# A decoder trunk in fp32: seven raw weight buffers instead of five, norm sums by transposing the squares, and another order of the program

## The chip, the cores and the metric

One core of one Trainium2 chip runs one program. The time is that of the device, in microseconds, from launch to the last byte of the output; 360.67 us is the median of three runs before the change (360.07 to 362.04).

## What is computed

Two layers of a decoder on 256 tokens of width 1024, all in fp32. The first mixes tokens by block attention (with 256 tokens and blocks of 256 it is plain causal attention), the second by three sparse branches: compressed keys, selected blocks, and a window (here the last two cover every earlier token). Each mixer is gated by a SiLU path, and after each layer an embedding is projected, gated by a sigmoid and added.

```python
for i in range(DEPTH):                       # DEPTH = 2
    h = rms_norm(x, norm_gain[i])
    if i % N_MIXERS == 0:
        x = x + moba_layer(h, moba_w_in[j], ..., moba_w_out[j], pos)
    else:
        x = x + nsa_layer(h, nsa_w_in[j], ..., nsa_cmp_w1[j], nsa_cmp_w2[j], nsa_w_out[j], pos)
    gate = jax.nn.sigmoid(rms_norm(x, ple_gate_gain[i]) @ ple_w_gate[i])
    x = x + gate * (p[i] @ ple_w_proj[i])
...
def rms_norm(x, gain):
    y = xf * lax.rsqrt(jnp.mean(xf * xf, axis=-1, keepdims=True) + NORM_EPS)
```

## The kernel before, in words

The residual stream lies in `xT`, eight tiles of 128 features by 256 tokens. A product in fp32 is made of three matmuls in a 32-bit format with a shorter mantissa: each operand is split into a rounded `hi` and a rest `lo`, and hi·hi + hi·lo + lo·hi is summed. For weights `split` (L490) does that: a DMA brings 512 KB (a granule, 128 x 1024) into a `raw` buffer, ScalarE writes `hi`, VectorE writes `lo = raw - hi`; there are five buffers each for raw, hi and lo (L21). A raw buffer comes free when its lo is made, a hi or lo when its matmuls are done. For activations `split_act` (L502) makes `a` from `xT`. A `Unit` (L517) is a product of 512 columns over eight such tiles, in four granules.

The sum over features of the squares, for the norm, is in class `Norm` (L592): ScalarE squares `xT`, VectorE adds the squares up in `sqacc`; `finish` (L617) then multiplies `sqacc` by a column of ones on TensorE, which sums over the 128 partitions and puts tokens on partitions, VectorE makes `ms` of it, GpSimd raises it to the power -1/2 (`rstd`), and two transposes spread that over partitions (`bc`). There are three such norms: `a` (first layer), `b` (its embedding gate), `c` (second layer).

Attention: a pair of heads has steps `A` (queries and keys transposed), `S` (scores: matmuls into two banks `s`, then on VectorE mask, scale and row extreme, which frees the bank, and the exponential on ScalarE), `T` (probabilities scaled, transposed on TensorE, copied) and `V` (times values). In the second layer the steps of group g are `gA`, `gS0` to `gS3`, `gT0` to `gT3`, `gV`; the compressed branch multiplies windows (`KC`, `KD`) by weights `in_w` in the four steps `W0` to `W3`, straight from raw buffers without a split, so that two raw buffers stay taken from the load (`w:W0`) until the step's matmuls are done.

The order. `PROGRAM` (L25) lists the steps; this is the order in which instructions are recorded and buffers of a kind are dealt out, so a load that stands early takes its buffer early. `Plan.schedule` (L264) then puts the recorded instructions into one order per engine with costs of its own (`cost`, L187; `SWITCH` for a change of TensorE's tiling, `POW` for GpSimd's power), and each engine executes its queue in that order. Nearly every instruction is emitted at L400, so the profile is read by tiles. SP issues almost all DMAs; `x0` to `x7` load the tiles of the input, `w:c0` to `w:c7` and `w:d0` to `w:d3` the first weights (eight tiles of the query's, four of the key's, 256 KB each), `consts` the constants and head gains, and `tk`, `tq` build the rotary tables from them on VectorE.

Of the kernel before, what the change touches and what calls it, by code (L numbers as in the profile page):

```python
# [7 lines left out]
F32 = mybir.dt.float32  # L8
F32R = mybir.dt.float32r
AF = mybir.ActivationFunctionType  # L10
OP = mybir.AluOpType
AX = mybir.AxisListType

P = 128
T = 256
D = 1024
KT = 8
HD = 64
EPS = 1e-6
SWITCH, POW = 150.0, 2300.0  # L20
NRAW, NHI, NLO, NPT, NA = 5, 5, 5, 9, 9  # L21
WARM = 16
MARGIN = 100.0

PROGRAM = ("w:c0 w:d0 x0 c0 x1 w:c1 w:d1 d0 c1 x2 x3 d1 w:c2 x6 w:d2 x4 x5 w:c3 w:c4 consts tk w:c5 tq w:c6 w:d3 x7 c2 a.1  "  # L25
# [21 lines left out]

WIDE = ('no',)

# [59 lines left out]
class Plan:  # L109
# [77 lines left out]
    def cost(self, op, views, first):  # L187
        n = first.elems() if isinstance(first, View) else 0
        e, m = op.engine, op.method
        if m == "dma_start":  # L190
            v = first if isinstance(first, View) else op.args[1]
            return v.elems() * 4 * v.ap.ap[0][1]
        if e == "tensor":
            k, c = op.args[1].ap.ap[0][1], op.args[1].ap.ap[1][1]
            op.mode = tuple(128 if x > 64 else 64 if x > 32 else 32 for x in (k, c))
            if m == "transpose":
                return 109.2
            if op.args[1].ap.dtype == mybir.dt.bfloat16:
                return n / 2.4
            if op.args[1].ap.dtype == F32R:  # L200
                return (n + 32) / 2.4 if n > 128 else 110

            tiles = 128 // op.mode[1] if op.mode[0] == 128 else 1
            return 2 * max(109.2 / tiles, 2 * n / 2.4 / tiles)
        if e == "gpsimd":
            if op.kwargs.get("op") == OP.pow:
                return (POW if n < 16 else 1300.0) + 130.0 * n
            return 100 + 2.3 * n
        psum = any(self.tags[v.tile.tag]["psum"] for v in views)
        rows = first.ap.ap[0][1]  # L210
        half = 110 if rows in (60, 64) and (any(v.box()[0] != first.box()[0] for v in views)
                                            or psum and first.ap.dtype == F32R and m == "activation") else 0
        if e == "scalar":
            if first.tile.tag == "early":
                return 1500.0
            c = (60 if psum else 110) + 0.833 * max(n, op.args[1].elems())
            return half + c + 93 * sum(isinstance(op.kwargs.get(k), View) for k in ("scale", "bias", "accum_out"))
        if m == "tensor_tensor_reduce":
            return 130 + 1.04 * n
        if m == "reciprocal":  # L220
            return 65 + 6.9 * n
        if m == "tensor_reduce":
            return 65 + 1.04 * op.args[1].elems()
        two = len([v for v in views if v.elems() > 2 and v is not first]) > 1
        if not psum and not two and m in ("tensor_copy", "tensor_scalar"):
            return 70 + half + 0.52 * n + 60 * any(isinstance(x, View) and x.elems() == 1 for x in op.args[2:])
        if m == "tensor_tensor" and args_step(op.args[1]) >= 16:
            return 65 + 1.75 * n
        return 65 + half + 1.055 * n + (65 if m == "scalar_tensor_tensor" and isinstance(op.args[2], View) else 0)
# [192 lines left out]
def trunk(ctx: ExitStack, tc: tile.TileContext, a, out):  # L422
# [3 lines left out]
    nc = Plan(tc.nc, {"sb": sb, "psum": psum})  # L426
# [8 lines left out]
    consts, wpool, apool, work = Pool(1), Pool(5), Pool(NA), Pool(2)  # L435
# [26 lines left out]
    ident, mask, valid, rmask = cs("ident"), cs("mask"), cs("valid"), cs("rmask")  # L462
# [7 lines left out]
    nc.vector.memset(warm, 0.0)  # L470
    neg_half = consts.tile([P, 16], F32, name="neg_half")
    nc.vector.memset(neg_half, -0.5)
    ones = consts.tile([P, 2], F32, name="ones")
    nc.vector.memset(ones, 1.0)

    def tables(name, gain, gains):
        t = work.tile([P, 2, 2, len(gains), HD], F32, tag=name[:2] + str(len(gains)), name=name, bufs=1)
# [114 lines left out]
    class Norm:  # L592
# [24 lines left out]
        def finish(self):  # L617
            ps = bank("tr", 2)
            for t in range(2):
                nc.tensor.matmul(ps[:, 2 * t:2 * t + 2], self.acc[:, 0, t * P:t * P + P], ones, start=True, stop=True)  # L620
            self.ms = work.tile([P, 2], F32, tag="ms", name="ms")
            nc.vector.tensor_scalar(self.ms, ps[:, 0:4:2], 1.0 / D, EPS, op0=OP.mult, op1=OP.add)
            self.rstd = work.tile([P, 2], F32, tag="rstd", name="rstd")
            nc.gpsimd.tensor_tensor(self.rstd, self.ms, neg_half[:, :2], op=OP.pow)
            self.e2 = work.tile([P, 2, 2], F32, tag="e2", name="e2")
            nc.vector.tensor_scalar(self.e2[:, 0], self.ms, 64 * EPS, None, op0=OP.mult)
            nc.vector.tensor_scalar(self.e2[:, 1], self.ms, EPS, None, op0=OP.mult)
            ps = bank("tr", 2)
            for t in range(2):
                nc.tensor.transpose(ps[:, t * P:t * P + P], self.rstd[:, t:t + 1].to_broadcast([P, P]), ident)  # L630
            self.bc = work.tile([P, T], F32, tag="bc", name="bc", bufs=1)
            nc.copy(self.bc, ps[:, :T])
# [230 lines left out]
    ps = bank("tr", 2)  # L863
# [4 lines left out]
    x0 = {}  # L868
# [185 lines left out]
    for k in (1, 3, 5, 6, 7):  # L1054
        todo[f"a.{k}"] = lambda k=k: nc.hold_on(lambda: n0.add(k), at["consts"])
    todo.update(a=n0.finish, consts=consts_, masks=masks_, tq=lambda: tab.update(q=tables("tq0", gmoba, [0])),
                tk=lambda: tab.update(k=tables("tk0", gmoba, [1])))
# [8 lines left out]
    x1, n2 = {}, Norm()  # L1066
# [11 lines left out]
    c2 = consts.tile([124, 2, HD], F32, name="c2")  # L1078
# [8 lines left out]
    def tabs2():  # L1087
# [4 lines left out]
                ntk=lambda: tab1.update(k=tables("tk1", gnsa, [2, 3])))  # L1092
# [304 lines left out]

    groups = [Group(g, f" {g}b" not in PROGRAM) for g in range(4)]
    for h, x in enumerate(halves1):
# [7 lines left out]
    for g in range(4):  # L1407
# [3 lines left out]
                KD0=lambda: KD(0), KD1=lambda: KD(1))  # L1411
# [6 lines left out]

    for step in PROGRAM.split():

        name, _, g = step.partition("/")
# [109 lines left out]
```

## Time and profile before

| | before |
|---|---|
| median of 3 runs | 360.67 us |
| the profiled execution | 362.55 us |
| its span | 360.7 us |
| TensorE matmuls / weight loads busy | 98% / 86% |
| VectorE, ScalarE, GpSimd busy | 89%, 75%, 7% |
| granted TensorE clock | 1.00 |
| moved by DMA | 58.95 MB, 163 GB/s |

PE and PEld are TensorE's matmuls and its weight loads, DVE is VectorE, ACT ScalarE, POOL GpSimd, SP the engine that issues DMAs. In groups and timelines a row reads: output tile <- input tiles, shape, count; behind the bar the busy time, the mean of one, and the engine's idle time ahead. `mm`, `s` and `tr` are banks of the accumulator memory. The profiled execution shows the span of the program's instructions; 1.85 us of its time lie around it.

### The profile page before, as it was taken

To read this page: it belongs to the slowest core of one execution; us is meant where nothing else is said; L and a number is where in the kernel's file an instruction comes from. 1 tells how busy PE (TensorE), PEld (TensorE's weight loads), DVE (VectorE), ACT (ScalarE), POOL (GpSimd) and SP (SyncE) were. 2 spreads that over 40 slices of the span, in tenths; PEclk is the share of its full clock that TensorE was granted. 3 is DMA by queue.
4 is the path that set the end of the run, shared out by engine and by line. 5 is a ranking of instruction groups with operands and counts; after the bars stand their busy time and mean duration, and the time that the engine had idled before them with its cause. 6 is when DMAs were issued, how large, how long until landed. Compare 5 with 4: busy or idle time off the path is not lost.

```text
span 360.7 us, 6783 instructions
## 1 busy us (share of the span) xinstructions
PE 353.6 (98%) x2397; PEld 311.2 (86%) x2397; DVE 321.7 (89%) x779; ACT 269.5 (75%) x594; POOL 25.9 (7%) x22
## 2 busy tenths in 40 slices
PE   8999999999999999999999999999999999999995
PEld 6788888989989999999889988876998888888884
DVE  4989999999999967969999989999899999878744
ACT  4867499886989966736664978987998999855731
POOL 1013300330000000000003200003000000000000
PEclk9999999999999999999999999999999999999999
DMA  7997657654533334644553664138834331136003
GB/s 226 321 367 255 196 194 271 195 177 121 171 119 116 119 118 124 224 148 149 171 164 125 231 203 150 62 109 298 300 128 160 109 125 59 60 115 224 12 6 113
DMA packets 20770, 58.95 MB, mean 163 GB/s; under 512 B 2560, under 2 KB 5632, under 8 KB 20736
## 3 DMA queue, kind: packets, MB, share of 16 engines
q1 hardware_dynamic: 20160, 58.04, 48.6%
q10 hardware_dynamic: 576, 0.48, 0.4%
q8 instruction: 19, 0.31, 0.3%
q14 instruction: 15, 0.12, 0.1%
HBM read 57.46 MB, written 1.05 MB: 162 GB/s over the span
## 4 chain that ended last, share of the span: by engine, by line
PE 72%; DVE 13%; ACT 6%; DMA 6%; issue 2%; SPq 0%; DVEq 0%; ACTq 0%
PE mm L400 55%; PE tr L400 10%; PE s L400 7%; DVE sm L400 3%; DVE lo L400 3%; DVE big L400 2%; ACT hi L400 2%; DVE hl L400 2%; DMA raw<-in_nsa_in 2%; DMA tmp<-in_moba_in 1%; DMA xT<-in_x 1%; DMA raw<-in_w 1%; DVE tmp L400 1%; ACT sm L400 1%; ACT pt L400 1%
## 5 line engine op out<-in xcount | busy, mean ns | idle before, releaser
L400 PE MATMUL mm<-hi,a 128*128 128x512 f32 (+2 forms) x448 | 128.7, 377 | 0.6 <-ACT hi L400 0.6
L400 ACT ACTIVATE hi<-raw 128x1024 fp32r<-128x1024 f32 (+2 forms) x98 | 97.5, 1007 | 37.3 <-PE mm L400 28.5
L400 DVE TENSOR_TENSOR lo<-raw,hi 128x1024 fp32r<-128x1024 f32 (+2 forms) x98 | 112.7, 1162 | 12.6 <-ACT hi L400 11.9
L400 PE MATMUL mm<-a,hi 128*128 128x256 f32 (+1 forms) x608 | 120.0, 293 | 0.0
L400 PEld LDWEIGHTS mm<-a,hi 128*128 128x128 f32 x608 | 95.5, 191 | 2.6 <-issue 0.6
L400 PEld LDWEIGHTS mm<-hi,a 128*128 128x128 f32 x448 | 79.7, 190 | 13.9 <-ACT hi L400 1.8
L400 PE MATMUL mm<-a,lo 128*128 128x256 f32 x320 | 87.8, 286 | 0.0
L400 PE MATMUL mm<-lo,a 128*128 128x512 f32 (+2 forms) x224 | 79.4, 372 | 0.0
L400 PEld LDWEIGHTS mm<-a,lo 128*128 128x128 f32 x320 | 59.9, 191 | 1.0
L400 PEld LDWEIGHTS mm<-lo,a 128*128 128x128 f32 x224 | 41.6, 188 | 7.3 <-DVE lo L400 0.7
L400 ACT ACTIVATE sm<-sm,nb 128x128 f32<-128x128 f32 (+1 forms) x96 | 42.8, 449 | 4.9 <-DVE nb L400 4.7
L400 DVE CUSTOM_DVE_ANT_0 sm<-s,cst,nr_q 128x128 f32<-128x128 f32 (+1 forms) x96 | 36.5, 411 | 1.2 <-PE s L400 0.7
L400 ACT ACTIVATE pt<-tr 128x384 f32<-128x384 f32 x48 | 22.0, 483 | 3.5 <-PE tr L400 3.2
L400 PE MATMUL tr<-cst,sm 128*128 128x128 f32 x144 | 23.3, 275 | 0.0
L400 POOL TENSOR_TENSOR r_q<-r,neg_half 128x16 f32<-128x16 f32 x5 | 14.6, 2922 | 83.5 <-DVE r L400 83.5
L400 PEld LDWEIGHTS tr<-cst,sm 128*128 128x128 f32 x144 | 17.0, 140 | 2.8 <-issue 0.8
L400 DVE TENSOR_SCALAR sm<-sm,l 128x128 f32<-128x128 f32 (+1 forms) x67 | 18.4, 317 | 0.3
L400 ACT ACTIVATION_READ_ACCUMULATOR sm<-sm,nb 128x1 f32 x96 | 18.4, 191 | 0.0
L400 ACT ACTIVATE a<-xT,gain_in 128x256 fp32r<-128x256 f32 x31 | 14.4, 497 | 5.1 <-DMA xT<-in_x 2.9
L400 DVE TENSOR_TENSOR hl<-tr,hl 64x512 fp32r<-64x512 f32 x24 | 16.5, 688 | 1.2 <-ACT qk_0r L400 0.4
L400 POOL TENSOR_TENSOR rstd<-ms,neg_half 128x2 f32<-128x2 f32 x4 | 2.8, 698 | 203.2 <-DVE ms L400 203.2
L400 PE MATMUL tr<-pt,v 128*64 128x256 f32 (+1 forms) x192 | 16.9, 328 | 0.0
(196 smaller groups left out, 475.8 us busy)
## 6 DMA issues: line engine op xcount, KB each, us to landing
raw<-in_moba_in SPq DMA_DIRECT2D x26, 512.0 KB, 4.4
raw<-in_nsa_in SPq DMA_DIRECT2D x24, 512.0 KB, 3.6
raw<-in_w_out SPq DMA_DIRECT2D x16, 512.0 KB, 3.5
raw<-in_ple_gate SPq DMA_DIRECT2D x16, 512.0 KB, 3.8
raw<-in_w SPq DMA_DIRECT2D x8, 512.0 KB, 3.5
raw<-in_ple_proj SPq DMA_DIRECT2D x4, 512.0 KB, 3.8
tmp<-in_moba_in SPq DMA_DIRECT2D x6, 256.0 KB, 4.7
raw<-in_nsa_vs SPq DMA_DIRECT2D x4, 304.0 KB, 3.1
```

The costliest lines, as they stand in the source:

```text
L400: getattr(getattr(self.nc, o.engine), o.method)(*[real(x) for x in o.args], **{k: real(x) for k, x in o.kwargs.items()})
```

## The change

Three edits: raw buffers go from five to seven; the norm sums are made by two transposes of the squares and a VectorE sum along the row; and `PROGRAM` is another order of the same steps, scheduled with two other costs.

```diff
-SWITCH, POW = 150.0, 2300.0
-NRAW, NHI, NLO, NPT, NA = 5, 5, 5, 9, 9
+SWITCH, POW = 165.0, 420.0
+NRAW, NHI, NLO, NPT, NA = 7, 5, 5, 9, 9
...
-PROGRAM = ("w:c0 w:d0 x0 c0 x1 w:c1 w:d1 d0 c1 x2 x3 d1 w:c2 x6 w:d2 x4 x5 w:c3 w:c4 consts tk w:c5 tq w:c6 w:d3 x7 c2 a.1  "
+PROGRAM = ("w:c0 x0 w:d0 x1 x3 consts w:c1 w:d1 x2 w:c2 x4 a.1 w:c3 c0 c1 x5 d0 tk c2 w:c4 tq w:c5 a.3 x6 w:c6 x7 w:c7 w:d3  "
...
             if op.kwargs.get("op") == OP.pow:
-                return (POW if n < 16 else 1300.0) + 130.0 * n
+                return POW + 148.0 * n
...
-    ones = consts.tile([P, 2], F32, name="ones")
-    nc.vector.memset(ones, 1.0)
...
             for t in range(2):
-                nc.tensor.matmul(ps[:, 2 * t:2 * t + 2], self.acc[:, 0, t * P:t * P + P], ones, start=True, stop=True)
+                nc.tensor.transpose(ps[:, t * P:t * P + P], self.acc[:, 0, t * P:t * P + P], ident)
             self.ms = work.tile([P, 2], F32, tag="ms", name="ms")
-            nc.vector.tensor_scalar(self.ms, ps[:, 0:4:2], 1.0 / D, EPS, op0=OP.mult, op1=OP.add)
+            nc.vector.tensor_reduce(self.ms, ps[:, :T].rearrange("p (t d) -> p t d", t=2), axis=AX.X, op=OP.add)
+            nc.vector.tensor_scalar(self.ms, self.ms, 1.0 / D, EPS, op0=OP.mult, op1=OP.add)
```

Three places show the order. Rows name output <- inputs; a tile's number is its buffer's, and since the tile of ones is gone, the same buffer often has a number lower by one in the change.

**The start, on SP.** First its issues before the change, from the program's first on (`tmp` and `raw` are buffers for weights; `cst` and `gmoba` the constants and head gains):

```order
L400 DMA xT_63<-in_x 128x256
L400 DMA tmp_82<-in_moba_in 128x256
L400 DMA tmp_85<-in_moba_in 128x512
L400 DMA xT_63<-in_x 128x256
L400 DMA tmp_86<-in_moba_in 128x512
L400 DMA xT_63<-in_x 128x256 x4
L400 DMA tmp_82<-in_moba_in 128x512
L400 DMA tmp_83<-in_moba_in 128x512
L400 DMA xT_63<-in_x 128x256
L400 DMA tmp_85<-in_moba_in 128x512
L400 DMA raw_128<-in_moba_in 128x512
L400 DMA cst_65<-in_cst 128x384
```

And with the change, from the same place:

```order
L400 DMA xT_63<-in_x 128x256
L400 DMA tmp_81<-in_moba_in 128x256
L400 DMA tmp_84<-in_moba_in 128x512
L400 DMA xT_63<-in_x 128x256 x2
L400 DMA cst_65<-in_cst 128x384
L400 DMA gmoba_66<-in_head_gain 128x256
L400 DMA tmp_85<-in_moba_in 128x512
L400 DMA xT_63<-in_x 128x256
L400 DMA tmp_81<-in_moba_in 128x512
```

The constants stand sixth instead of fifteenth, and the weights d1 (`tmp_86`, now `tmp_85`) and the tiles of x beyond the third come behind them. On VectorE the same place, with the change, from the second tile of x on:

```order
L400 SCALAR_TENSOR_TENSOR a_1_119<-xT_63,gain_in_64,a_1_119 128x256
L400 TENSOR_TENSOR lo_116<-tmp_83,hi_111 128x512
L400 SCALAR_TENSOR_TENSOR a_2_120<-xT_63,gain_in_64,a_2_120 128x256
L400 TENSOR_TENSOR tk_0_127<-cst_65,gmoba_66 128x128 x2
L400 TENSOR_TENSOR tq_0_135<-cst_65,gmoba_66 128x128 x2
L400 TENSOR_TENSOR lo_117<-tmp_85,hi_112 128x512
```

The four products of the tables stand ahead of the lo of d1 (last row); before, they stood behind it and the lo of four further tiles.

**The scores of the second layer's group 0, on PE.** Before, from the fourth score step of group 0 (`s <- k_0r`) to the first of group 1 (`s <- k_1r`):

```order
L400 MATMUL s_158<-k_0r,hl_151 128x256 x2
L400 MATMUL mm_79<-hi_110,a_3_122 128x512
L400 MATMUL s_159<-k_0r,hl_151 128x512
L400 MATMUL tr_75<-cst_65,sm_70 128x128 x3
L400 MATMUL tr_76<-cst_65,sm_71 128x128 x3
L400 MATMUL s_159<-k_0r,hl_151 128x512
L400 MATMUL mm_79<-hi_110,a_3_122 128x512
L400 MATMUL mm_79<-lo_115,a_3_122 128x512
L400 MATMUL mm_78<-hi_110,a_3_122 128x512 x2
L400 MATMUL mm_78<-lo_115,a_3_122 128x512
L400 MATMUL s_158<-k_1r,hl_150 128x256 x2
```

With the change, the last rows ahead of group 1's first score step (16 rows with 24 matmuls of 256 columns stand between group 0's third score step and these):

```order
L400 MATMUL tr_74<-cst_65,sm_71 128x128 x3
L400 MATMUL tr_75<-cst_65,sm_69 128x128 x3
L400 MATMUL mm_79<-hi_109,a_4_122 128x512 x2
L400 MATMUL mm_79<-lo_114,a_4_122 128x512
L400 MATMUL mm_78<-hi_109,a_4_122 128x512 x2
L400 MATMUL mm_78<-lo_114,a_4_122 128x512
L400 MATMUL mm_79<-hi_109,a_7_125 128x512 x2
L400 MATMUL mm_79<-lo_114,a_7_125 128x512
L400 MATMUL mm_78<-hi_109,a_7_125 128x512 x2
L400 MATMUL mm_78<-lo_114,a_7_125 128x512
L400 MATMUL s_160<-k_1r,hl_152 128x256 x2
```

The projections `mm` that lie between two score steps are another share of the same work: more of it stands here, less later.

**The weights of the compressed branch, on SP.** Before, around the first two loads from `in_w` (step `w:W1`):

```order
L400 DMA raw_131<-in_ple_proj 128x1024
L400 DMA raw_132<-in_w 128x1024
L400 DMA raw_128<-in_w 128x1024
L400 DMA raw_129<-in_w_out 128x1024
L400 DMA raw_130<-in_ple_proj 128x1024
L400 DMA raw_131<-in_w_out 128x1024
L400 DMA raw_129<-in_moba_in 128x1024
L400 DMA raw_130<-in_w_out 128x1024
```

With the change, around the same two loads, which come 17 issues later:

```order
L400 DMA raw_131<-in_ple_gate 128x1024
L400 DMA raw_132<-in_w 128x1024
L400 DMA raw_133<-in_w 128x1024
L400 DMA raw_134<-in_ple_gate 128x1024
L400 DMA raw_128<-in_ple_gate 128x1024
L400 DMA raw_129<-in_nsa_in 128x1024
L400 DMA raw_130<-in_nsa_in 128x1024
L400 DMA raw_131<-in_nsa_in 128x1024
L400 DMA raw_134<-in_nsa_in 128x1024
```

From these loads until W1's matmuls all other weights pass through three raw buffers before (129, 130, 131) and through five with the change (128 to 131 and 134).

42 rows, old and new, of the table PROGRAM are left out of this document.

## The prediction

> **What bounds the kernel now.** First the page: span, engines, and the chain that ended last.
>
> ```profile
> span 360.7 us, 6783 instructions
> PE 353.6 (98%) x2397; PEld 311.2 (86%) x2397; DVE 321.7 (89%) x779; ACT 269.5 (75%) x594; POOL 25.9 (7%) x22
> PE 72%; DVE 13%; ACT 6%; DMA 6%; issue 2%; SPq 0%; DVEq 0%; ACTq 0%
> ```
>
> TensorE (PE) has work nearly all the time, and 72% of the chain is its own. A busy PE can still lose time, since ends of matmuls are modelled. So I read starts, in the timeline of PE and of its weight loads (PEld), where group 0 of the second layer's attention begins:
>
> ```profile
> 214.00 0.40 PE L400 MATMUL mm<-a,hi 128*128 128x256 f32 x2
> 214.24 0.28 PE L400 MATMUL mm<-a,lo 128*128 128x256 f32 x1
> 214.79 0.50 PE L400 MATMUL s<-k_0r,hl 128*128 128x256 f32 x2 [0.27 <-DVE nb L400]
> ...
> 214.78 0.30 PEld L400 LDWEIGHTS s<-k_0r,hl 128*128 128x128 f32 x2 [0.47 <-DVE nb L400]
> ```
>
> Two 256-wide matmuls start within 0.24 us, so one is issued every 0.12. After 214.24 the next came 0.55 later: 0.43 lost, and PEld's wait says 0.47. PEld's waits are therefore a good measure of what PE loses. The view of waits, PEld alone, gives them by stretch: 0 to 25, then 100 to 135, then 200 to 285 us.
>
> ```profile
> PEld mm L400 <- ACT hi L400: 1.5, 2, 0.9
> PEld mm L400 <- DVE lo L400: 0.5, 2, 0.2
> ...
> PEld s L400 <- DVE nb L400: 0.4, 1, 0.4
> PEld mm L400 <- DVE tmp L400: 0.2, 1, 0.2
> PEld mm L400 <- DVE l L400: 0.2, 1, 0.2
> ...
> PEld s L400 <- DVE nb L400: 2.7, 8, 0.5
> PEld mm L400 <- DMA raw<-in_w: 0.6, 1, 0.6
> PEld s L400 <- DVE pc L400: 0.3, 1, 0.3
> PEld tr L400 <- ACT sm L400: 0.2, 1, 0.2
> PEld s L400 <- DVE big L400: 0.2, 1, 0.2
> ```
>
> That is 2.0 us at the start, 0.8 at the end of the first attention, 4.0 in the second: 6.8 us in all that an order could win. The rest is matmuls that no line of the change removes. In the last stretch PE waits for VectorE (DVE) to free a bank of scores ("nb" ends a block of the softmax). The windows say how full DVE is there (columns: PE, PEld, DVE, ACT, POOL busy, clock, DMA):
>
> ```profile
> 200.00:220.00 20.00, 19.42 (x155) 18.72 (x153) 18.55 (x37) 16.36 (x34) 0.65 (x1) 1.00 0.63 211
> 220.00:240.00 20.00, 19.74 (x111) 16.11 (x110) 19.65 (x70) 18.50 (x59) 0.00 (x0) 1.00 0.24 81
> 240.00:260.00 20.00, 19.81 (x171) 15.15 (x170) 17.96 (x48) 17.13 (x43) 3.16 (x2) 1.00 0.77 270
> 260.00:280.00 20.00, 19.79 (x160) 18.31 (x159) 19.14 (x67) 18.07 (x48) 0.75 (x1) 1.00 0.43 153
> 280.00:300.00 20.00, 20.00 (x161) 16.60 (x162) 19.89 (x70) 19.79 (x59) 0.00 (x0) 1.00 0.33 106
> ```
>
> From 200 to 300 DVE works 18.55+19.65+17.96+19.14+19.89 = 95.2 of 100 us: a second limit, 4.8 us behind the first. The granted clock is 1.00 in every row.
>
> **The change part by part.** Kinds and counts of instructions stay the same, but for the norms and some copies that pass between DVE and ScalarE (ACT). So the change is worth waits, not work.
>
> *Norm sums, three times.* Rows: the products with ones, transposes of the same tile size, and the DVE reduction of 256 elements.
>
> ```profile
> L400 PE MATMUL tr<-ones,sqacc 128*128 128x2 f32 x12 | 1.6, 223 | 0.0
> L400 PE MATMUL tr<-cst,rstd 128*128 128x128 f32 x6 | 1.1, 272 | 0.0
> L400 DVE TENSOR_REDUCE cm<-pc 128x16 f32<-128x256 f32 x4 | 1.7, 416 | 0.0
> L400 DVE COPY big<-tmp 64x510 f32<-64x510 f32 x4 | 1.7, 422 | 0.1
> ```
>
> Four records of PE per norm become two, at half the busy time (12 for 1.6 us against 6 for 1.1, partly overlapped): I take -0.1 us each, -0.3 together; the ends are -0.5 (all 1.6 less 1.1) and 0. DVE gains three reductions, 3 x 0.42 = 1.25 us. The order hands two of the four "big" copies to ACT, -0.84, and a few small copies and casts more, so DVE's sum stays about level; I cost it at nothing. Without that cover, 1.25 us would fall on DVE. The Trainium skill (VectorE: DVE Perf Modes, section "Rules for kernel authors") speaks against this edit: it calls the reduction the slowest VectorE operation and advises restructuring. The rows agree: 416 ns for 256 elements, where the copy does 510 in 422; by either the cost is the 1.25 us above.
>
> *The start.* Rows: the first 20 us, the transfers that move forward, the tables that need them, two lo, SP's sixth to ninth issue, and three 512-wide matmuls that start within 0.68 us (0.227 each).
>
> ```profile
> 0.00:20.00 20.00, 18.31 (x82) 14.13 (x83) 14.87 (x37) 12.71 (x25) 1.01 (x7) 1.00 0.86 287
> cst<-in_cst SPq DMA_DIRECT2D x1, 192.0 KB, 5.4
> gmoba<-in_head_gain SPq DMA_DIRECT2D x1, 128.0 KB, 5.2
> 15.85 0.49 DVE L400 TENSOR_TENSOR tk<-cst,gmoba 128x128 f32<-128x128 f32 x2
> 8.58 1.29 DVE L400 TENSOR_TENSOR lo<-tmp,hi 128x512 fp32r<-128x512 f32 x2
> 3.34 1.75 SPq L400 DMA_DIRECT2D xT<-in_x  x4
> ...
> 25.62 0.62 PE L400 MATMUL mm<-hi,a 128*128 128x512 f32 x2
> 26.07 0.39 PE L400 MATMUL mm<-lo,a 128*128 128x512 f32 x1
> 26.30 0.62 PE L400 MATMUL mm<-hi,a 128*128 128x512 f32 x2
> ```
>
> SP now issues the constants (192 + 128 KB) as sixth and seventh, ahead of weights d1 and of x2; at 287 GB/s that is 1.1 us of transfer put in front of them. On DVE the four table products stand ahead of d1's lo instead of behind it and four more. Two 512-wide lo take 1.29, so 0.65 each. SP's sixth to ninth issue took from 3.34 to 5.09, so the constants go out by about 3.9 and land near 9 (3.9 + 5.2); the tables run from about 9.5 to 10.3, d1's lo to 11.0, and d1's matmuls end near 11.5 instead of 11.0. Behind it weights c2, c3 and c4 land in time at before's rate, and the ten tiles c0 to c7, d0, d1 are done near 20.3, where before had ten and a half (a tile is six matmuls of 0.227, 1.36 us). I take +0.3; ends -1.5 (PE's 2.0 largely gone, since c4 to c7 now come without cst between them) and +2.1 (rival below).
>
> *The end of the first attention* (0.8 lost). By the order, counted in PE work ahead, pair 3's transposes move from 90 to 67 us, so VectorE reaches this stretch with less left, and V2 and V3, which wait for its last probabilities, stand 1.4 us later. I take -0.6 of the 0.8; ends -0.8 and +0.5 (one more bank wait of 0.4 to 0.5).
>
> *Scores of the second attention* (4.0 lost). Each score step fills both banks, and DVE must empty them before the next:
>
> ```profile
> L400 DVE CUSTOM_DVE_ANT_0 sm<-s,cst,nr_q 128x256 f32<-128x256 f32 x48 | 22.3, 477 | 0.0
> L400 DVE CUSTOM_DVE_ANT_0 sm<-s,cst,nr_q 128x128 f32<-128x128 f32 x48 | 16.3, 345 | 1.2 <-PE s L400 0.7
> L400 DVE DVE_READ_ACCUMULATOR2_ANT nb<- 128x1 f32 x96 | 8.0, 84 | 0.0
> 242.75 4.87 DMA raw<-in_w
> ...
> L400 SPq DMA_DIRECT2D raw<-in_w x2: 327/328/328, 81.5 to 86.3; - x2
> ```
>
> That is 2 x 0.477 + 2 x 0.345 + 4 x 0.084 = 2.0 us of DVE, and other DVE work stands between. Counting PE's rows from one score step to the next (0.12 per 256-wide, 0.227 per 512-wide, 0.1 per transpose), before had distances of 3.3, 4.7, 4.4, 2.7, 7.0, 2.1 and 13.2 us for groups 0 and 1; now 3.9, 3.6, 6.9, 4.0, 8.6, 7.8, 4.8. The two that hardly cover DVE's 2.0 are gone. The order counts say how far this goes: at group 3's second transposes PE's and DVE's work ahead are as before, so the stretch as a whole is no lighter for DVE, and what can be won is bounded by its idle 4.8 and PE's 4.0.
>
> *Buffers.* The row of 4.87 is a pair of compression weights (W2) that PE waited 0.6 for: W1's two transfers, now moved back, had sat in two of five raw buffers since 81.5 and 86.3 us (last row), and W2's could be issued only when W0's matmuls had freed theirs, 4.7 us of PE work ahead. Now five of seven cycle and 7.0 us lie between, against 4.87 plus 0.4 of issue: that 0.6 goes. hi and lo keep five buffers each, so splits run no further ahead. Buffers and scores together: -1.9, about half of 4.0, since PE that runs early finds DVE nearly full at 280 to 300. Ends: -4.0 and 0.
>
> *Sum.* The profiled execution took 362.55 us (span 360.7, 1.85 around it): 362.55 + 0.3 - 0.6 - 1.9 - 0.3 = 360.05, that is -2.5. Against the median of 360.67, which is 1.9 below that execution, **358.2 us**. The measurement tells about 0.5% (1.8 us) from no change.
>
> **The rivals.** *VectorE takes the gain back.* At 280 to 300 it is 99% full, and its work up to there is the same; if its idle time does not shrink, the -1.9 becomes 0: 360.67 + 0.3 - 0.6 - 0.3 = 360.1. For it: that window. Against: 0.6 was a transfer, and DVE's 2.0 us of idle in 240 to 260 follow the stalls. The Trainium skill (Perfetto Trace Analysis, section "Identifying the Most-Contended Engine") judges TensorE by weight loads instead of matmuls; by it DVE's 89% stands above 86%, so this rival would be the likeliest. PE's start spacing here speaks the other way: outside the waits it is at its constant 0.12.
>
> *The start starves: slower.* DVE works in order, so lateness of the constants passes to d1's lo, and every tile behind. It decides at about 9.5 us, when DVE reaches the tables. With 1.1 us of transfer in front and the four products (1.0) not covered, +2.1, and nothing won elsewhere: 362.8. For it: ten tiles instead of ten and a half already. Against: constants issued at 3.9 need 5.2.
>
> *The change doesn't do what it says:* raw buffers come free at lo as before, lo at hi, hi at PE; earlier transfers then feed nothing: 360.7.
>
> *More is won:* both later waits go entirely, -0.8 - 4.0 - 0.3 = -5.1: 355.6.
>
> **How the numbers follow.** Forecast 0.42, VectorE 0.25, starving 0.18, nothing 0.05, more 0.10. The forecast's own range is 357.0 to 359.6, so some fifth of it lies above 358.87 (-0.5%). Faster: 0.10 + 0.34 + 0.03 of the VectorE case = 0.47; same: 0.08 + 0.22 + 0.05 = 0.35; slower 0.18. Range 355.5 to 362.5: it reaches the large win and most of the starved start, leaving 2 in 10 out.
>
> **What would show it.** PEld's wait for "nb" in the second attention near 1.5 instead of 2.7, and none for raw<-in_w; DVE 200 to 300 above 96 us busy: forecast. Same waits moved to 280 to 320: VectorE rival. DVE idle at 9 to 11 us on cst or gmoba, PE's first waits above 3 us: starving. I am wrong outright if PE waits for raw transfers after 25 us.

## The result, and the profile after

| | before | after |
|---|---|---|
| median | 361.09 us (9 runs) | 359.32 us (9 runs) |
| lowest to highest | 360.07 to 362.04 | 358.42 to 359.96 |
| ratio, 95% interval | | 0.9949 (0.9934 to 0.9964) |
| the profiled execution | 362.55 us | 358.42 us |

The change is worth 1.8 us, 0.5%. The two profiled executions lie 4.1 us apart, because that of before is above all nine of its timed runs and that of after is the fastest of its nine. A difference between these two pages is therefore not yet an effect of the change; the experiments sort that out.

First the page of after, its span, its busy times and its chain by engine:

```profile
span 356.6 us, 6777 instructions
...
PE 351.0 (98%) x2391; PEld 309.7 (87%) x2391; DVE 321.0 (90%) x775; ACT 273.2 (77%) x600; POOL 26.6 (7%) x22
...
PE 96%; DMA 1%; DVE 1%; POOL 0%; SPq 0%; issue 0%; ACT 0%; DVEq 0%; ACTq 0%
```

The chain was 72% TensorE and 13% VectorE; now it hardly leaves TensorE. The view of waits, PEld alone, from 200 to 285 us, answers to the last rows of before (engine, tile, what it waited for: us, times, longest):

```profile
PEld s L400 <- DVE nb L400: 0.5, 2, 0.2
PEld s L400 <- DVE l L400: 0.4, 1, 0.4
PEld tr L400 <- DVE sm L400: 0.4, 1, 0.4
PEld s L400 <- DVE pc L400: 0.3, 1, 0.3
PEld s L400 <- DVE lo L400: 0.2, 1, 0.2
```

That is 1.8 us where before had 4.0: "nb" fell from 2.7 to 0.5, the wait for raw<-in_w is gone, and two waits of 0.4 are new. One wait stands at a place where before had none, 135 to 165 us:

```profile
PEld tr L400 <- POOL rstd L400: 0.6, 1, 0.6
```

The windows of the second attention (columns as before):

```profile
200.00:220.00 20.00, 20.00 (x152) 19.07 (x151) 19.63 (x42) 16.69 (x35) 0.00 (x0) 1.00 0.68 232
220.00:240.00 20.00, 20.00 (x130) 15.66 (x129) 19.52 (x65) 17.87 (x51) 0.00 (x0) 1.00 0.38 130
240.00:260.00 20.00, 20.00 (x177) 17.36 (x175) 19.36 (x63) 19.85 (x55) 3.15 (x2) 1.00 0.70 266
260.00:280.00 20.00, 19.97 (x165) 17.39 (x164) 19.52 (x69) 18.45 (x52) 0.54 (x1) 1.00 0.35 107
280.00:300.00 20.00, 20.00 (x152) 16.94 (x151) 19.86 (x71) 19.81 (x60) 0.00 (x0) 1.00 0.24 79
```

VectorE is busy 97.9 of these 100 us instead of 95.2, and 2.1 us of idle time are left. Not all of that rise is the new order's: held_both and held_buffers below, which keep the old order, show 96.9.

### The profile page after: what moved, and what is told of

Read it like the earlier page. It is cut to its first block, busy times and chain, and to the rows that moved or that the text cites. A ratio compares the mean times of both kernels' runs of the same rounds, so it can differ in the third digit from the quotient of the medians.

```text
span 356.6 us, 6777 instructions
## 1 busy us (share of the span) xinstructions
PE 351.0 (98%) x2391; PEld 309.7 (87%) x2391; DVE 321.0 (90%) x775; ACT 273.2 (77%) x600; POOL 26.6 (7%) x22
## 4 chain that ended last, share of the span: by engine, by line
PE 96%; DMA 1%; DVE 1%; POOL 0%; SPq 0%; issue 0%; ACT 0%; DVEq 0%; ACTq 0%
PE mm L400 73%; PE tr L400 14%; PE s L400 9%; DMA tmp<-in_moba_in 1%; POOL rstd L400 0%; SPq L400 0%; DVE big L400 0%; DVE ms L400 0%; DVE hi L400 0%; ACT tmp L400 0%; DVEq L1525 0%; ACTq L400 0%
## 5 line engine op out<-in xcount | busy, mean ns | idle before, releaser
L400 PE MATMUL mm<-lo,a 128*128 128x512 f32 (+2 forms) x224 | 80.8, 373 | 0.0
L400 PE MATMUL tr<-cst,sm 128*128 128x128 f32 x144 | 24.5, 275 | 0.0
L400 POOL TENSOR_TENSOR rstd<-ms,neg_half 128x2 f32<-128x2 f32 x4 | 3.7, 926 | 191.2 <-DVE ms L400 116.0
```

The costliest lines, as they stand in the source:

```text
L400: getattr(getattr(self.nc, o.engine), o.method)(*[real(x) for x in o.args], **{k: real(x) for k, x in o.kwargs.items()})
```

## The experiments

### One part at a time, planned again: a surprise

The first four kernels take the three edits apart (norm sums, buffers, order with its costs) and let the planner make its schedule anew.

```diff
 norm_only, against before
+                nc.tensor.transpose(ps[:, t * P:t * P + P], self.acc[:, 0, t * P:t * P + P], ident)
+            nc.vector.tensor_reduce(self.ms, ps[:, :T].rearrange("p (t d) -> p t d", t=2), axis=AX.X, op=OP.add)
 buffers_only, against before
-NRAW, NHI, NLO, NPT, NA = 5, 5, 5, 9, 9
+NRAW, NHI, NLO, NPT, NA = 7, 5, 5, 9, 9
 order_only, against before
+SWITCH, POW = 165.0, 420.0
+PROGRAM = ("w:c0 x0 w:d0 x1 x3 consts w:c1 w:d1 x2 w:c2 x4 a.1 w:c3 c0 c1 x5 d0 tk c2 w:c4 tq w:c5 a.3 x6 w:c6 x7 w:c7 w:d3  "
 old_norm, against the changed kernel
+                nc.tensor.matmul(ps[:, 2 * t:2 * t + 2], self.acc[:, 0, t * P:t * P + P], ones, start=True, stop=True)
```

> The kernel before with the new norm sums alone (order list, costs and five raw buffers as before). Theory of the prediction: three times two fewer matmul records with ones, -0.3 us (ends -0.5 and 0), DVE's 1.25 us for the reductions hidden: 360.8 against a before of 361.1, ratio 0.998 to 1.000. Rival, the reduction falls on DVE where DVE is the limit: +0.5 to +1.25 us, ratio 1.0015 to 1.0035. Second rival, that the norm matters more than was thought (what follows a norm waits for it): below -0.8 us, ratio under 0.998.

> The kernel before with seven raw buffers alone. Theory of the prediction: only the wait for raw<-in_w (0.6 us of PEld) can go, since hi and lo keep five buffers: 0 to -0.6 us, ratio 0.998 to 1.000, and no PEld wait for raw<-in_w in the trace. Rival, buffers carry the gain: -1.2 to -1.8 us, ratio 0.995 to 0.9967, and the waits for nb shrink too.

> The kernel before with the new order list and its two costs alone, five raw buffers, products with ones. Theory of the prediction: the score waits and the end of the first attention go, a transfer wait may stay: -0.8 to -1.4 us, ratio 0.996 to 0.998; PEld's waits for nb near 0.5 us. Rival, the order needs seven buffers: PE waits for raw transfers after 25 us, time at or above before, ratio 1.000 to 1.005.

> The changed kernel with the products with ones put back. Theory of the prediction: the norm is worth 0.3 us, so -1.5 us of the change's -1.8 stay, ratio to before 0.995 to 0.997. Rival, the reduction costs VectorE what the order won there: faster than the changed kernel, -2.3 to -3 us, ratio 0.9915 to 0.9937. Second rival, the norm carries the gain: -0.3 to -0.8 us, ratio 0.998 to 0.999.

Measured ratios to before (361.2 us): norm_only 1.0516 (1.0491 to 1.0541), buffers_only 1.046 (1.0432 to 1.0488), order_only 1.0266 (1.0244 to 1.0289), old_norm 1.0175 (1.015 to 1.02). All lie outside every expectation: 6.5 to 19 us are lost in all four. This can't be read as the price of a part, because each of these edits made the planner choose anew at many places. In norm_only, PEld in the timeline and the windows show what a bad choice costs:

```profile
127.29 0.50 PEld L400 LDWEIGHTS mm<-a,hi 128*128 128x128 f32 x2 [2.31 <-ACT a L400]
...
216.52 0.50 PEld L400 LDWEIGHTS mm<-hi,a 128*128 128x128 f32 x2 [5.85 <-issue]
```

```profile
126.00:130.00 4.00, 2.71 (x11) 2.52 (x12) 4.00 (x13) 3.70 (x12) 0.00 (x0) 0.63 0.47 155
216.00:224.00 8.00, 7.45 (x40) 7.48 (x41) 4.69 (x14) 2.69 (x6) 0.00 (x0) 0.59 0.12 42
```

Two waits of 2.3 and 5.9 us end in these windows, whose granted clock is 0.63 and 0.59, so that such a wait is paid a second time. What follows from these runs is only that each of these settings, planned anew, got a worse order. To price them, the order has to stand still.

### The order held

In all further kernels `schedule` is replaced: it replays, engine by engine, the order that the planner made for before or for after. Where raw buffers change in number they are dealt out as they come free; where the norm changes, the reduction goes directly ahead of `ms`. Without an edit the replay issues each engine the same instructions in the same order.

```diff
     def schedule(self):
+        rows, slots = json.loads(zlib.decompress(base64.b64decode(PIN)))
...
+            queues.setdefault(e, []).append((pos, o))
...
+            free = {t: list(range(len(x["real"]))) for t, x in self.tags.items()}
```

> The kernel before with every engine's order held as it is, and only the norm sums changed (two transposes for two products, a reduction put ahead of ms, no tile of ones). Theory of the prediction: -0.3 us on PE (ends -0.5 and 0), DVE's 1.25 us hidden: ratio to before 0.9985 to 1.000. Rival, the chain of each norm grows by the reduction's 0.42 us, and PE waits for it three times: +0.3 to +1.2 us, ratio 1.001 to 1.0035.

> The kernel before with every engine's order held as it is, and only the raw buffers raised from five to seven, dealt out in turn. Theory of the prediction: the one wait for raw<-in_w (0.6 us) goes, nothing else: -0.3 to -0.6 us, ratio 0.998 to 0.999. Rival, seven buffers carry the gain: -1.2 us or more, ratio under 0.9967. Second rival, nothing happens (raw comes free at lo, and earlier transfers feed nothing): ratio 0.9993 to 1.0007.

> The changed kernel with every engine's order held, and only the norm sums put back to products with ones. Theory of the prediction: 0.3 us slower than the changed kernel (0 to 0.5), ratio to before 0.995 to 0.9965. Rival, the reduction lengthens the chain of a norm where PE waits for it: 0.4 to 1 us faster than the changed kernel, ratio 0.992 to 0.994.

> The changed kernel with every engine's order held, and only five raw buffers, so that SP issues a load later where no buffer is free. Theory of the prediction: the new order parks W1's pair late, so at most the 0.6 us wait for a transfer comes back: ratio to before 0.9945 to 0.997. Rival, the new order needs the seven buffers: PE waits for raw transfers, or for hi and lo behind them, 1.5 us or more in all, ratio to before 0.999 or above.

| kernel | order | raw | norm | ratio to before, 95% | median |
|---|---|---|---|---|---|
| held_norm | old | 5 | new | 0.9978 (0.9962 to 0.9994) | 360.53 |
| held_buffers | old | 7 | old | 0.9944 (0.9925 to 0.9963) | 359.57 |
| held_ones | new | 7 | old | 0.9918 (0.9895 to 0.9941) | 358.54 |
| held_five | new | 5 | new | 1.0415 (1.0385 to 1.0446) | 376.80 |

Before was 361.5 us beside them.

**Norm sums in the old order: -0.8 us** (0.2 to 1.4 by the interval, so the 0.3 of the theory isn't excluded; the growing chain of the rival is). PEld in the timeline at the first norm, of before and of held_norm, shows the size:

```profile
20.58 0.64 PEld L400 LDWEIGHTS tr<-ones,sqacc 128*128 128x128 f32 x4
21.13 0.30 PEld L400 LDWEIGHTS mm<-hi,a 128*128 128x128 f32 x2
```

```profile
19.49 0.37 PEld L400 LDWEIGHTS tr<-cst,sqacc 128*128 128x128 f32 x2
19.83 0.30 PEld L400 LDWEIGHTS mm<-hi,a 128*128 128x128 f32 x2
```

From the first record to the next matmul's: 0.55 us with ones, 0.34 with transposes, so 0.21 at this norm, and about 0.63 if all three save as much.

**Seven buffers in the old order: -2.0 us**, as much as the whole change, where the theory had 0.3 to 0.6 (the rival's figure held, but not its shrinking "nb": 1.7 us from 200 to 285, as in held_norm). The reason is in the weights of the compressed branch. PEld in held_norm, then in held_both (below), which differs from it by the buffers alone:

```profile
242.33 1.97 PEld L400 LDWEIGHTS mm<-raw,big 128*60 128x60 f32 x18
245.59 1.48 PEld L400 LDWEIGHTS mm<-raw,big 128*60 128x60 f32 x14 [1.29 <-DMA raw<-in_w]
```

```profile
242.59 3.27 PEld L400 LDWEIGHTS mm<-raw,big 128*60 128x60 f32 x32
```

With five buffers TensorE stops for 1.29 us in the middle of these 32 matmuls (0.65 in the profiled execution of before); with seven they run through. The rest of the 2.0 I can't place; held_norm against held_both gives 0.9978 to 0.9938, 1.4 us, which is about that wait.

**The old norm sums in the new order: 0.9918, no slower than the changed kernel** (0.9949 above, 0.9931 below, each against its own before). The theory had 0.3 us slower; the sign is the rival's. So the 0.8 us that the norm sums bring in the old order are not there in the new one. Beside held_buffers, which differs from it by the order alone, held_ones also prices the order with the old norm sums: 359.57 to 358.54, -1.0 us, though the two intervals overlap.

**The new order with five buffers: +15.3 us.** This is not the gain less one part: the order doesn't fit five buffers. The loads for W0, W3 and W2 now follow closely: of the first four, three are out by 232.8 us, and the fourth goes out only at 243.3, while matmuls on the compression weights run (from 241.3) and free a buffer. SP, ACT and PEld in the timeline of held_five:

```profile
227.03 16.61 SPq L400 DMA_DIRECT2D raw<-in_w  x4
...
248.21 1.06 ACT L400 ACTIVATE hi<-raw 128x1024 fp32r<-128x1024 f32 x1 [8.06 <-DMA raw<-in_nsa_in]
...
252.72 0.18 PEld L400 LDWEIGHTS tr<-cst,sm 128*128 128x128 f32 x1 [7.59 <-ACT sm L400]
```

From the first to the fourth of these issues SP spends 16.6 us, a split's weights come late, ScalarE stands 8.06 us at that hi, and behind it in its queue stands the probability that TensorE then waits 7.59 us for. So here a late buffer reached TensorE through an engine's queue, not as a wait for a transfer. This wait is half of the 15.3; the rest is not followed up.

### Both parts in the old order, the new wait, and VectorE's room

The wait for rstd has a suspect: GpSimd's power took 1.61 us there, and 0.70 at each of the other three powers of 128x2 in that run. VectorE, GpSimd and PEld in the timeline of after:

```profile
157.28 0.17 DVE L400 TENSOR_SCALAR ms<-ms 128x2 f32<-128x2 f32 x1
157.36 1.23 DVE L400 TENSOR_TENSOR lo<-raw,hi 128x1024 fp32r<-128x1024 f32 x1
158.50 0.23 DVE L400 TENSOR_SCALAR e<-ms 128x2 f32<-128x2 f32 x2
...
157.53 1.61 POOL L400 TENSOR_TENSOR rstd<-ms,neg_half 128x2 f32<-128x2 f32 x1 [71.53 <-DVE ms L400]
...
159.19 0.19 PEld L400 LDWEIGHTS tr<-cst,rstd 128*128 128x128 f32 x2 [0.58 <-POOL rstd L400]
```

The power ends at 159.14, 0.55 behind the end of lo (157.36 + 1.23), as if most of its 0.70 had run only then. fix_b puts the two small products e ahead of that lo:

```diff
 VectorE's queue at norm b, from ms on
 TENSOR_SCALAR ms<-ms 128x2
+TENSOR_SCALAR e<-ms 128x2 x2
 TENSOR_TENSOR lo<-raw,hi 128x1024
-TENSOR_SCALAR e<-ms 128x2 x2
```

held_both is before with seven buffers and the new norm, order held; after_again the changed kernel as it is; more_vector adds, in `Group.scores`,

```diff
+            nc.vector.tensor_tensor(cst[:, 128:384], cst[:, 384:640], cst[:, 512:768], op=OP.add)
             self.S[h] = sm, l
```

> The kernel before with every engine's order held, and both seven raw buffers and the new norm sums. If the two gains measured apart (ratios 0.9978 and 0.9944 to before) come from different places, they add: ratio 0.991 to 0.9935, below the changed kernel's 0.9949, and then the new order gives no gain of its own. Rival, they overlap (one wait that both remove): 0.9935 to 0.996. Theory of the prediction (order worth 1.3 us by itself): the changed kernel stays 1 us or more ahead of this one.

> The changed kernel itself, instruction for instruction, beside the others on the same chip. Ratio to before 0.9934 to 0.9964 as measured. If the rstd of 1.61 us at norm b comes from the order (VectorE's subtraction lo, which reads two tiles of on-chip memory, stands right behind ms), it shows again, 1.4 us or more; if it was chance, 0.70.

> The changed kernel with one swap on VectorE: at norm b the two small products e stand ahead of the subtraction lo, which stood right behind ms, so that GpSimd's power starts ahead of lo. Theory that lo blocks the power: rstd 0.70 instead of 1.61 us, lo waits or takes 0.7 longer instead, PE's wait for rstd (0.6) goes, 0.3 to 0.6 us faster than the changed kernel in the same call. Rival, the power was slow by chance: no difference (within 0.2 us). Second rival, the delayed lo is waited for by PE: nothing won or up to 0.3 us lost.

> The changed kernel with order held and 16 more VectorE sums of 128x256 in the second layer's attention, one behind each score step, whose result is read by nothing: by the rows of 421 ns, 16 x 0.36 to 0.42 = 5.8 to 6.7 us of VectorE. Theory of the prediction (TensorE the bound, VectorE a second limit with 2.1 us idle from 200 to 285 us and 4.8 from 285 to 325): 1.5 to 4 us slower than the changed kernel. Rival, VectorE sets the pace there: 5.5 us or more slower. Second rival, VectorE has room: 0.7 us or less.

| kernel | ratio to before (361.57), 95% | median |
|---|---|---|
| held_both | 0.9938 (0.9921 to 0.9956) | 359.18 |
| after_again | 0.9931 (0.9910 to 0.9951) | 358.79 |
| fix_b | 0.9920 (0.9899 to 0.9941) | 358.48 |
| more_vector | 1.0044 (1.0026 to 1.0061) | 363.13 |

**The order by itself is worth 0.4 us (359.18 to 358.79), which these intervals can't tell from nothing.** held_both lies on the border between its two cases (adding 0.991 to 0.9935, overlapping 0.9935 to 0.996), so this run doesn't tell them apart; but the 1 us that the theory wanted between it and the changed kernel isn't there. With the old norm sums the same order brought 1.0 (above); the 0.6 between the two is as long as the wait for rstd, which only the new order and the new sums together have. What else became of the order's gain, the waits of PEld show. held_both first, from 200 to 285 us:

```profile
PEld s L400 <- DVE nb L400: 1.7, 6, 0.5
...
PEld s L400 <- DVE pc L400: 0.3, 1, 0.3
PEld tr L400 <- ACT sm L400: 0.2, 1, 0.2
PEld mm L400 <- DVE lo L400: 0.2, 1, 0.2
PEld s L400 <- DVE big L400: 0.2, 1, 0.2
```

That is 2.6 us against the 1.8 of after: -0.8, of "nb" alone -1.2, with l and sm taking 0.8. Then the rows "issue" of the whole execution, waits that no engine's work explains, of held_both and of after_again:

```profile
PEld tr L400 <- issue: 1.2, 4, 0.4
PEld mm L400 <- issue: 1.2, 4, 0.4
```

```profile
PEld mm L400 <- issue: 1.8, 5, 0.4
...
PEld tr L400 <- issue: 0.7, 4, 0.2
...
PEld s L400 <- issue: 0.4, 2, 0.2
```

2.4 against 2.9: +0.5. With -0.6 at the end of the first attention (0.8 in every kernel of the old order, 0.2 in every one of the new), -0.2 behind 285 us (0.6 to 0.4) and +0.6 for rstd, the order sums to -0.8 - 0.6 - 0.2 + 0.6 + 0.5 = -0.5 us, close to the measured 0.4. The start is left out of this sum, since its waits scatter by 1 us among kernels of one order (below).

**The slow power is the order's.** It took 1.61 us again in after_again, held_five and more_vector, the other kernels with the new sums and the new order as it is. In fix_b, VectorE and GpSimd:

```profile
157.57 0.26 DVE L400 TENSOR_SCALAR e<-ms 128x2 f32<-128x2 f32 x2
157.75 2.48 DVE L400 TENSOR_TENSOR lo<-raw,hi 128x1024 fp32r<-128x1024 f32 x2
...
157.62 0.69 POOL L400 TENSOR_TENSOR rstd<-ms,neg_half 128x2 f32<-128x2 f32 x1 [71.53 <-DVE ms L400]
```

The power starts first and takes 0.69, and PE has no wait for it. The time fell by 0.3 us to 358.48, the fastest median of these four and 0.8% below before; that it is faster than the changed kernel the intervals don't prove. held_ones never had this wait: its `ms` came without the reduction, and the power began ahead of lo. At 0.9918 it is no slower than fix_b, so even with the wait gone no gain of the norm sums shows in the new order. At its first norm, held_ones has the same effect in small, VectorE and GpSimd:

```profile
18.49 0.69 DVE L400 TENSOR_TENSOR lo<-tmp,hi 128x512 fp32r<-128x512 f32 x1
...
18.65 1.09 POOL L400 TENSOR_TENSOR rstd<-ms,neg_half 128x2 f32<-128x2 f32 x1 [17.11 <-DVE ms L400]
```

A lo half as long had begun ahead, the power took 1.09, and it ended 0.56 behind that lo.

**VectorE is nearly as full as TensorE.** The 16 sums show in the groups of more_vector, and one of them in its timeline; then the window 200 to 285 of after_again and of more_vector:

```profile
L400 DVE TENSOR_TENSOR cst<-cst 128x256 f32<-128x256 f32 x16 | 6.8, 423 | 0.0
```

```profile
278.50 0.09 DVE L400 DVE_READ_ACCUMULATOR2_ANT nb<- 128x1 f32 x1
278.50 0.42 DVE L400 TENSOR_TENSOR cst<-cst 128x256 f32<-128x256 f32 x1
278.83 1.22 DVE L400 TENSOR_TENSOR lo<-raw,hi 128x1024 fp32r<-128x1024 f32 x1
```

```profile
200.00:285.00 85.00, 84.97 (x645) 73.87 (x644) 82.89 (x248) 77.80 (x202) 4.13 (x4) 1.00 0.52 180
```

```profile
200.00:285.00 85.00, 83.72 (x627) 71.36 (x626) 83.56 (x250) 75.07 (x196) 3.71 (x3) 1.00 0.50 173
```

The busy times of the sums add up to 6.8 us, but they overlap other instructions: by starts, a sum pushes the next instruction back by 0.33 (278.50 to 278.83), and VectorE's busy time in the whole execution grew by 5.1 us (321.4 to 326.5). These 5.1 cost 4.3 us of time (363.13 less 358.79), so only 0.8 were absorbed, less than the 2.1 that VectorE had idle in this stretch. The 4.3 lie a little above the theory's 4 and below the rival's 5.5, but the rival's figure was set for 5.8 to 6.7 us of added work; for 5.1 it would be lower. So this run doesn't tell which of the two engines sets the pace: most of what VectorE is given comes out as time.

## Why the prediction came out, point by point

The time and the sign were right: 2.5 us less were forecast, 1.8 and 2.5 (0.9949 and 0.9931) measured. For TensorE as the bounding engine speaks the chain of after, 96% its own; more_vector shows VectorE to be almost as much of a limit. The terms are less good than their sum, and that the sum came out is in part luck: the order, forecast at -1.6 (start, end of the first attention, scores), brought 0.4 to 1.0, and the buffers, forecast at -0.6, brought 1.4 to 2.0.

- *Start, +0.3.* PEld's waits in the first 25 us were 2.0, 1.5, 1.9 and 1.0 in four executions of the old order and 1.4, 2.0, 1.7 and 1.3 in four of the new, both 1.6 on average; more_vector, a fifth of the new, had 0.5. The term is zero within that scatter. It was not tried by itself. Nothing starved: the tables ran at 8.6 us, as early as hoped.
- *End of the first attention, -0.6.* Right for the waits that the prediction counted (0.8 to 0.2 in every profile), but in the same stretch "issue" rose from 0.2 to 0.6.
- *Scores and buffers, -1.9.* The sum holds, the split doesn't. **The step that was mis-sized is "that 0.6 goes" for the buffers**: seven buffers alone bring 1.4 to 2.0. The 0.6 was read from one execution, and the same wait is 1.3 in another; of the 2.7 for "nb", 1.0 was also of that execution, since the three other executions of the old order show 1.7. The scores brought 0.8 after the new waits for l and sm, where 1.3 was forecast.
- *Norm sums, -0.3.* Mis-sized on TensorE: I took 0.1 each from overlapping busy times, where the starts give 0.21. Against it stands a cost that the prediction put at nothing: a reduction ahead of `ms` that is 0.42 us longer lets the power begin behind a lo, +0.6 in the new order. Together they come to nothing there: held_ones, without the new sums, is no slower than the changed kernel. The rule of the Trainium skill on reductions (VectorE: DVE Perf Modes, section "Rules for kernel authors") named the right operation, though the cost that showed here was its place in a chain, not VectorE's time.
- The rivals: *VectorE takes the gain back* did not happen (waits for named engines behind 285 us fell from 0.6 to 0.4), but more_vector shows how near it is. By the rule of the Trainium skill that went with it, the limit would be VectorE (90% against 87%). The chain of after, 1% VectorE, speaks against that; the 4.3 us lost of 5.1 added don't. *Doesn't do what it says* fell with held_buffers. *More is won* would have needed all of the waits; the changed kernel keeps 1.8 us of them in the second attention.

Of what was to show it: "nb" 0.5 instead of the 1.5 forecast, no wait for raw<-in_w, VectorE 97.9 (above 96), no wait for raw transfers on TensorE. Two of these signs don't tell the order from the buffers: held_buffers, in the old order, has no wait for raw<-in_w either, and VectorE at 96.9.

## What to carry to other kernels

A list that orders the work is fitted to buffers, costs and instructions together: price an edit with the order held, since a planner that runs anew answers another question. Read a wait's size from several executions before it becomes a term, and count starts, not busy times, where an engine is pipelined. When a chain grows by a short step, look at which long instruction now starts ahead of the next engine's.

## What the runs showed of the hardware

- GpSimd's power of 128x2 took 1.61 us where a VectorE subtraction of two tiles in on-chip memory, 1.23 long, had begun ahead of it (four runs), and 1.09 behind one of 0.69 (held_ones). The 51 other powers of this size in the fourteen runs took 0.70 to 0.71, also where another VectorE operation had begun ahead, such as a reduction `ssq <- tmp` of 0.69. The Trainium skill (SBUF — State Buffer, section "SBUF: two separate sides") says that such an instruction and a GpSimd one exclude each other for their whole length, whichever starts first. The first direction agrees: in these cases the power ended 0.55 to 0.56 us behind lo. The other does not show: in fix_b lo began 0.13 us behind the power, and both lo together took 2.48 us, as two of 1.23 would; in before a lo that began 0.16 us behind a longer power (128x16, 2.91 us) took 1.22.
- A wait of TensorE of 2.3 us cost clock in one run and not in another. In norm_only the granted clock of the 4 us in which it ended was 0.63 (row above); in order_only a wait of the same length left 1.00, by PEld in the timeline and the windows at its end and after it:

```profile
211.93 0.30 PEld L400 LDWEIGHTS mm<-a,hi 128*128 128x128 f32 x2 [2.35 <-ACT v L400]
```

```profile
210.00:214.00 4.00, 2.07 (x16) 2.06 (x17) 3.94 (x5) 2.95 (x6) 0.00 (x0) 1.00 0.74 227
214.00:218.00 4.00, 4.00 (x25) 3.50 (x24) 3.35 (x8) 2.07 (x5) 0.00 (x0) 1.00 0.77 269
```

The Trainium skill (TensorE: Matmul & The Clock Gate, section "Why this matters for your kernels") asks for no idle gap above about 3 us; here the clock fell below full once already with one of 2.3.
